# One pool for the weights of a whole decoder layer, and the down projection's operands kept in DRAM as high and low halves

## The chip, the cores and the metric

The kernel runs on one core of a Trainium2 chip. Its time is the device time of one execution in microseconds. Before the change the median of three runs is 2220.11 us (2217.4 to 2222.4). The profiled execution of the same kernel took 2217.63 us, of which the profile's span covers 2215.9 us.

## The reference

One layer of a hybrid decoder on 512 tokens of width 2048, all in fp32. Cut to what matters:

```python
h = rmsnorm(x, attn_pre_norm)
proj = h @ w_in                               # 2048 -> gated linear attention + differential attention
m = concat(gla(proj), diff_attention(proj)) @ w_o
x = x + rmsnorm(m, attn_post_norm)
h = rmsnorm(x, ffn_pre_norm)
up = h @ w_ffn_in                             # 2048 -> 2 x 5632
a, b = up[..., :5632], up[..., 5632:]
a = conv_w[0]*a[t-2] + conv_w[1]*a[t-1] + conv_w[2]*a[t] + conv_b
f = (gelu(a) * b) @ w_ffn_out                 # 5632 -> 2048
x = x + rmsnorm(f, ffn_post_norm)
```

The change touches how the weights of all these products are staged, and above all how gelu(a) * b travels from the up projection to the down projection.

## The kernel before

**Three products for one.** An fp32 value is split into a high half (ScalarE, ACT, copies it into the shorter type fp32r) and a low half (VectorE, DVE, subtracts the high half). A product is then three TensorE (PE) products: high by high, high by low, low by high. Weights arrive in *granules* of 128x1024 (512 KB) on SyncE's queue (SP); `granule` (L102) turns each into a pair "whi" (ACT, L111) and "wlo" (DVE, L112). `split` (L123) does the same for the moving operand: ACT at L124, DVE at L125. The moving operand of all stages lies in two resident tiles, "ah" and "al".

**Stages.** The input projections with both attentions run until about 690 us, then the output projection, a passage whose order is written out by hand (`to_ffn`), and `first_pair`, which makes the first 512 columns of the feed-forward net. From about 966 us come 20 *up units* (10 column groups, the gate branch and the linear branch of each), from about 1740 us 10 *down units*, and from about 2159 us a last part that adds the product of the first 512 columns and finishes the layer.

**A unit** computes a 2x2 block product with seven block products in place of eight, from sums of blocks. Its seven segments are called x0, z0, y0, z1, x1, y1 and y2, and each uses two granules and one of seven moving operands: a11, s5, s2, s3, a12, s7, a22, in that order. A granule is 24 products of 128x256 in an up unit (L888 to L890) and 12 of 128x512 in a down unit (L985 to L987). The weight sums are made by DVE (L853, L871) and by accumulating DMAs that GpSimd (POOL) issues (`more`, L837). Weights of a unit come into tiles "rt" (first block, four buffers) and "raw" (four buffers).

**From up to down.** After each unit of the linear branch `product` (L941) multiplies the two branches and `token_sums` writes the seven moving operands of the down stage to DRAM ("sd"): three are parts of the product, four are sums. `prepare` loads one such operand into a tile "st" and splits it into its place in "ah" and "al"; the down stage has 35 of these. Down products are accumulated in "acc" and "accp" by `into` (L991 on ACT, L993 on DVE).

**Pools.** "w" holds raw (4 buffers), whi and wlo (4 each) until the end of `first_pair`. It is then closed, and "w2" (rt 4, raw 4, whi and wlo 3 each) is opened in the same region. The working tiles of the up stage lie in a pool "fa"; when it is closed, those of the down stage come into "ff", in the same place. A tile in a pool that lies over an earlier one has to wait until the last reader of what lay there is done.

**What sets the order.** Outside the passages written by hand a scheduler that runs with a model of the engines orders each engine's queue; an engine then executes its queue strictly in order, SP's and POOL's queues of DMAs too.

## Time and profile before

| what | value |
|---|---|
| median of three runs | 2220.11 us |
| profiled execution | 2217.63 us |
| its span | 2215.9 us |
| mean granted TensorE clock | 0.991 |
| PE busy | 2148.3 us (97%) |
| DVE busy | 1421.0 us (64%) |
| ACT busy | 903.5 us (41%) |
| moved by DMA | 303.83 MB, 137 GB/s |

PE is the engine for which all else works. A row of the page's groups has line, engine, operation, output and inputs, then the count, the total busy time, the mean duration in ns, and the idle time of the engine just before these instructions with what ended it. Rows of a timeline have the start in us, the duration, and in brackets the idle time before, with its releaser. A row of the windows has the stretch, its length, the busy time and number of instructions of PE, its weight loads, DVE, ACT and POOL, the granted clock, the DMA engines' busy share and the rate in GB/s.

### The profile page before, as it was taken

The numbers are of one execution on the slowest core, as the hardware profiler recorded it, in microseconds if no ns is written. First come the engines' busy times: TensorE is split into PE (matmuls) and PEld (weight loads), VectorE is DVE, ScalarE is ACT, GpSimd is POOL, SyncE is SP. The second block draws the span as 40 slices with busy tenths as digits, with TensorE's granted clock in tenths as the row PEclk, the third lists the DMA queues.
The fourth block names the chain that finished last, engine by engine and source line by source line (L and its number), as shares of the span: only waits on it lengthen the run. The fifth ranks groups of instructions, "written<-read, shape, count | busy, mean of one in ns | idle before, by whom it ended". The sixth has DMA issues, their size and how long they took to land.

```text
span 2215.9 us, 31875 instructions
## 1 busy us (share of the span) xinstructions
PE 2148.3 (97%) x13009; PEld 1896.9 (86%) x13009; DVE 1421.0 (64%) x1721; ACT 903.5 (41%) x1162; POOL 204.4 (9%) x245
## 2 busy tenths in 40 slices
PE   7999999999999999999999999999999699999997
PEld 6778888877888889789999999999999588777786
DVE  5345553444453245857786777878778577887887
ACT  4233332333342234334554444454454364444442
POOL 1000000000000000011111111110111010110101
PEclk9999999999999999989999999999999899999999
DMA  6322222222224344175767667576766776676654
GB/s 208 111 67 77 76 77 76 77 77 85 77 88 168 96 143 162 40 180 138 161 150 184 145 156 183 131 163 159 175 154 148 224 220 160 167 190 155 166 128 144
DMA packets 218471, 303.83 MB, mean 137 GB/s; under 512 B 11776, under 2 KB 155572, under 8 KB 216404
## 3 DMA queue, kind: packets, MB, share of 16 engines
q1 hardware_dynamic: 165204, 238.87, 33.2%
q0 software_dynamic: 53120, 62.92, 18.3%
q8 instruction: 102, 1.67, 0.3%
q14 instruction: 45, 0.37, 0.1%
HBM read 273.97 MB, written 27.79 MB: 136 GB/s over the span
## 4 chain that ended last, share of the span: by engine, by line
PE 76%; issue 15%; DMA 4%; DVE 3%; POOL 1%; ACT 1%; SPq 0%; POOLq 0%; DVEq 0%; ACTq 0%
PE bank L888 11%; PE bank L890 11%; PE bank L889 11%; PE bank L165 6%; PE bank L167 6%; PE bank L166 6%; PE bank L149 5%; PE bank L147 5%; PE bank L148 5%; DMA raw<-in_w_ffn_out_dram 2%; PE bank L414 1%; DVE wlo L112 1%; PE bank L482 1%; PE bank L513 1%; PE bank L986 1%
## 5 line engine op out<-in xcount | busy, mean ns | idle before, releaser
L112 DVE TENSOR_TENSOR wlo<-raw,whi 128x1024 fp32r<-128x1024 f32 x325 | 396.1, 1223 | 380.7 <-ACT whi L111 380.0
L111 ACT ACTIVATE whi<-raw 128x1024 fp32r<-128x1024 f32 x325 | 343.8, 1059 | 625.0 <-PE bank L167 162.4
L112 DVE TENSOR_TENSOR wlo<-rt,whi 128x1024 fp32r<-128x1024 f32 x240 | 291.9, 1222 | 114.8 <-ACT whi L111 114.1
L111 ACT ACTIVATE whi<-rt 128x1024 fp32r<-128x1024 f32 x240 | 253.2, 1059 | 272.7 <-PE bank L889 177.7
L888 PE MATMUL bank<-ah,whi 128*128 128x256 f32 x1280 | 354.9, 277 | 4.8 <-ACT whi L111 4.8
L890 PE MATMUL bank<-ah,wlo 128*128 128x256 f32 x1280 | 354.7, 277 | 0.5 <-DVE wlo L112 0.5
L889 PE MATMUL bank<-al,whi 128*128 128x256 f32 x1280 | 354.5, 277 | 0.0
L165 PE MATMUL bank<-whi,ah 128*128 128x512 f32 x616 | 246.3, 401 | 0.2 <-ACT ah L124 0.2
L888 PEld LDWEIGHTS bank<-ah,whi 128*128 128x128 f32 x1280 | 241.6, 189 | 5.3 <-ACT whi L111 5.2
L166 PE MATMUL bank<-wlo,ah 128*128 128x512 f32 x616 | 242.7, 395 | 0.2 <-DVE wlo L112 0.2
L167 PE MATMUL bank<-whi,al 128*128 128x512 f32 x616 | 242.1, 395 | 0.0
L890 PEld LDWEIGHTS bank<-ah,wlo 128*128 128x128 f32 x1280 | 241.4, 189 | 0.8 <-DVE wlo L112 0.8
L889 PEld LDWEIGHTS bank<-al,whi 128*128 128x128 f32 x1280 | 241.5, 189 | 0.0
L986 PE MATMUL bank<-wlo,ah 128*128 128x512 f32 x560 | 222.0, 396 | 11.3 <-DVE wlo L112 11.2
L985 PE MATMUL bank<-whi,ah 128*128 128x512 f32 x560 | 198.8, 394 | 21.6 <-ACT ah L124 18.7
L987 PE MATMUL bank<-whi,al 128*128 128x512 f32 x560 | 219.6, 392 | 0.0
L147 PE MATMUL bank<-ah,whi 128*128 128x512 f32 (+1 forms) x528 | 202.4, 383 | 0.0
L148 PE MATMUL bank<-al,whi 128*128 128x512 f32 (+1 forms) x528 | 201.6, 382 | 0.0
L149 PE MATMUL bank<-ah,wlo 128*128 128x512 f32 (+1 forms) x528 | 200.6, 380 | 0.4 <-DVE wlo L112 0.4
L985 PEld LDWEIGHTS bank<-whi,ah 128*128 128x128 f32 x560 | 105.3, 188 | 46.4 <-ACT ah L124 19.1
L986 PEld LDWEIGHTS bank<-wlo,ah 128*128 128x128 f32 x560 | 105.5, 188 | 42.3 <-DVE wlo L112 19.9
L167 PEld LDWEIGHTS bank<-whi,al 128*128 128x128 f32 x616 | 116.1, 188 | 26.2 <-DVE al L125 0.3
(241 smaller groups left out, 3836.3 us busy)
## 6 DMA issues: line engine op xcount, KB each, us to landing
raw<-in_w_in_dram SPq DMA_DIRECT2D x96, 512.0 KB, 3.9
raw<-in_w_ffn_in_dram SPq DMA_DIRECT2D x96, 512.0 KB, 5.3
raw<-in_w_ffn_out_dram SPq DMA_DIRECT2D x48, 512.0 KB, 6.8
rt<-in_w_ffn_in_dram SPq DMA_DIRECT2D x40, 512.0 KB, 5.9
rt<-in_w_ffn_in_dram POOLq DMA_DIRECT2D x40, 512.0 KB, 5.9
raw<-in_w_ffn_in_dram POOLq DMA_DIRECT2D x40, 512.0 KB, 7.0
raw<-in_w_o_dram SPq DMA_DIRECT2D x32, 512.0 KB, 3.7
rt<-in_w_ffn_out_dram SPq DMA_DIRECT2D x20, 512.0 KB, 7.7
```

The costliest lines, as they stand in the source:

```text
L111: act(hi, raw, AF.Copy)
L112: tt(lo, raw, hi.bitcast(F32), ALU.subtract)
L147: mm(o, wh, ah[:, t0:t1, kk, :], start=st, stop=False)
L148: mm(o, wh, al[:, t0:t1, kk, :], start=False, stop=False)
L149: mm(o, wl, ah[:, t0:t1, kk, :], start=False, stop=sp)
L165: mm(banks[t], ah[:, t, s, :], w[0][:, k, :], start=st, stop=False)
L166: mm(banks[t], ah[:, t, s, :], w[1][:, k, :], start=False, stop=False)
L167: mm(banks[t], al[:, t, s, :], w[0][:, k, :], start=False, stop=sp)
L888: mm(o, wh, sh[:, :, kk, :], start=start and kk == 0 and n == 0, stop=False, **NOW)
L889: mm(o, wh, sl[:, :, kk, :], start=False, stop=False, **NOW)
L890: mm(o, wl, sh[:, :, kk, :], start=False, stop=kk == HK - 1, **NOW)
L986: mm(b[j], sh[:, o:o + P], w[1][:, q, :], start=False, stop=False, **NOW)
```

## The change

There are four parts.

1. *One pool.* "w" stays open for the whole kernel, with three buffers each of whi and wlo. The tiles rt get a pool of their own, "rp", opened after the output projection. A few granules of the first stages go to spare tiles: one in the first half of the mixer, one more each in `to_ffn`.
2. *In the down stage every fourth granule* is split into a pair "xhi"/"xlo" (one buffer) in "ff".
3. *The operands are split when they are written.* `put` splits each of the seven operands through one pair of tiles "oh" and "ol" (one buffer each) and writes both halves: 14 stores of 256 KB per token_sums where there were 7. The sums are now made in place in two buffers, and the order of the seven is a11, s5, s2, s3, a12, s7, a22. `prepare` becomes two loads straight into ah and al, with no tile st and no split. s2 and s3 of the first group are prepared earlier than before.
4. *The residual rows* of the last part are loaded into parts of ah and al that are free by then.

```diff
-    wstack = ExitStack()
-    wpool = wstack.enter_context(tc.tile_pool(name="w", bufs=4, side="right"))
+    wpool = ctx.enter_context(tc.tile_pool(name="w", bufs=3))
...
-            w[g] = granule(None, 2, raws[g])
+            w[g] = granule(None, 2, raws[g], spare=mx if g == 3 else None, bufs=1)
...
-            w[g] = granule(w_o3[:, order[2 * g]:order[2 * g] + 2, 1536:2048], 2, spare=wp if g > 4 else None)
+            w[g] = granule(w_o3[:, order[2 * g]:order[2 * g] + 2, 1536:2048], 2, spare=wp if g > 3 else None)
...
-        weights_f(wa, 0, 3)
+        weights_f(wa, 0, 3, wp)
...
+    rp = ctx.enter_context(tc.tile_pool(name="rp", bufs=4))
...
-    sd = [{n: dram.tile([P, 2, S], F32, name=f"sd{c}{n}") for n in SN} for c in range(NG // 2)]
+    sd = [{n: [dram.tile([P, 2, S], F32, name=f"sd{c}{n}{v}") for v in "hl"] for n in SN} for c in range(NG // 2)]
...
-    wstack.close()
-    wpool = ctx.enter_context(tc.tile_pool(name="w2", bufs=3, side="right"))
 
     def load_t(src, a):
-        raw = wpool.tile([P, GR], F32, name="rt", tag="rt", bufs=4)
+        raw = rp.tile([P, GR], F32, name="rt", tag="rt", bufs=4)
...
-                hl = granule(None, self.a, raws[g])
+                turn[0] += 1
+                hl = granule(None, self.a, raws[g], spare=ff if ff and turn[0] % 4 == 0 else None, bufs=1)
...
         def put(n, src):
-            dma(sd[c][n][:, i, :].rearrange("p (n t) -> p n t", n=2), src)
-
-        def add(n, x, y, op):
-            t = fp.tile([P, 2, 256], F32, name=n, tag="sum", bufs=4)
-            tt(t, x, y, op)
-            put(n, t)
-            return t
+            hl = [fp.tile([P, 2, 256], F32R, name=f"o{v}", tag=f"o{v}", bufs=1) for v in "hl"]
+            split(hl[0], hl[1], src)
+            for d, v in zip(sd[c][n], hl):
+                dma(d[:, i, :].rearrange("p (n t) -> p n t", n=2), v.bitcast(F32))
+
+        def total():
+            return fp.tile([P, 2, 256], F32, name="sum", tag="sum", bufs=2)
 
         put("a11", a11)
+        s = total()
+        tt(s, a21, a22, ALU.subtract)
+        put("s5", s)
+        tt(s, s, a11, ALU.subtract)
+        put("s2", s)
+        tt(s, s, a12, ALU.add)
+        put("s3", s)
         put("a12", a12)
+        s = total()
+        tt(s, a11, a21, ALU.subtract)
+        put("s7", s)
         put("a22", a22)
...
-    def prepare(c, n, stage=None):
-        raw = stage or ff.tile([P, GR], F32, name="st", tag="st", bufs=2)
-        dma(raw, sd[c][n].rearrange("p g x -> p (g x)"))
-        split(piece(ah, *place[n]), piece(al, *place[n]), raw)
+    def prepare(c, n):
+        for v, d in zip((ah, al), sd[c][n]):
+            dma(piece(v, *place[n]).bitcast(F32), d.rearrange("p g x -> p (g x)"))
...
             downs = [down_unit(c, cb) for c in range(NG // 2) for cb in range(2)]
+            prepare(0, "s2")
             downs[0].x0()
+            prepare(0, "s3")
             u.y2()
...
-            x1[t] = ff.tile([P, D], F32, name="x1", tag="x1", bufs=2)
+        x1 = {t: v[:, h].rearrange("p k c -> p (k c)").bitcast(F32)
+              for t, (v, h) in enumerate(((ah, 1), (al, 1), (ah, 2), (al, 2)))}
```

**The order at the opening of the up stage.** ACT's queue there, as it was. s5h, s2h and s3h are operands of the up units, "p" is the first up unit's evacuated product, and each whi made from rt belongs to an up unit.

```order
L124 ACTIVATE s5h<-u 128x1024
L124 ACTIVATE ah<-u 128x1024 x2
L740 ACTIVATE u<-u 128x512
L124 ACTIVATE s2h<-u 128x1024
L124 ACTIVATE s3h<-u 128x1024
L111 ACTIVATE whi<-rt 128x1024 x2
L909 ACTIVATE p_7080<-bank 128x512
L111 ACTIVATE whi<-rt 128x1024 x4
```

And with the change:

```order
L123 ACTIVATE s5h<-u 128x1024
L110 ACTIVATE whi<-rt 128x1024
L123 ACTIVATE ah<-u 128x1024 x2
L740 ACTIVATE u<-u 128x512
L110 ACTIVATE whi<-rt 128x1024 x2
L123 ACTIVATE s2h<-u 128x1024
L110 ACTIVATE whi<-rt 128x1024 x2
L911 ACTIVATE p_7114<-bank 128x512
L123 ACTIVATE s3h<-u 128x1024
L110 ACTIVATE whi<-rt 128x1024
```

Three splits of rt stand ahead of s2h now, and two more ahead of s3h, where both came before any of them.

**The order in the up stage.** ACT's queue over the last segments of one unit of the linear branch and the first of the next, as it was; whi is a weight granule, "u" and "p" are evacuated products.

```order
L909 ACTIVATE p_10624<-bank 128x512
L111 ACTIVATE whi<-rt 128x1024 x3
L111 ACTIVATE whi<-raw 128x1024 x6
L111 ACTIVATE whi<-rt 128x1024
L919 ACTIVATE u<-bank 128x2x256
L111 ACTIVATE whi<-rt 128x1024 x2
L737 ACTIVATE u<-u,cols 128x512 x2
L111 ACTIVATE whi<-rt 128x1024
```

And with the change, where "oh" is the high half that `put` writes, from the part "u" or the sum "sum":

```order
L123 ACTIVATE oh<-u 128x512
L110 ACTIVATE whi<-raw 128x1024 x2
L123 ACTIVATE oh<-sum 128x512
L110 ACTIVATE whi<-raw 128x1024 x2
L123 ACTIVATE oh<-sum 128x512
L110 ACTIVATE whi<-raw 128x1024
L123 ACTIVATE oh<-sum 128x512
L110 ACTIVATE whi<-raw 128x1024
L110 ACTIVATE whi<-rt 128x1024
L921 ACTIVATE u<-bank 128x2x256
L123 ACTIVATE oh<-u 128x512
L110 ACTIVATE whi<-rt 128x1024 x2
```

Splits for the stores now stand one by one between the splits of the weights; two more follow, with one granule of rt between, so that ACT handles 10 granules between the first and the last of the seven.

**The order from the up to the down stage.** ACT's queue, as it was:

```order
L124 ACTIVATE ah<-u 128x1024
L111 ACTIVATE whi<-rt 128x1024 x6
L111 ACTIVATE whi<-raw 128x1024
L991 ACTIVATE accp_15927<-bank 128x512
L991 ACTIVATE accp_15928<-bank 128x512
L991 ACTIVATE acc_15925<-bank 128x512
L991 ACTIVATE acc_15926<-bank 128x512
L124 ACTIVATE ah<-st 128x1024 x2
```

And with the change:

```order
L110 ACTIVATE whi<-rt 128x1024 x5
L123 ACTIVATE oh<-u 128x512
L123 ACTIVATE oh<-sum 128x512 x3
L123 ACTIVATE oh<-u 128x512
L123 ACTIVATE oh<-sum 128x512
L123 ACTIVATE oh<-u 128x512
L998 ACTIVATE accp_16291<-bank 128x512
L998 ACTIVATE accp_16292<-bank 128x512
L110 ACTIVATE xhi<-rt 128x1024
L110 ACTIVATE whi<-rt 128x1024
L110 ACTIVATE whi<-raw 128x1024 x2
L123 ACTIVATE ah<-st 128x1024
```

The seven splits of the last token_sums stand together ahead of the first down products' evacuation (accp), and behind that comes a granule split into xhi. The split of "st" that remains is the last part's operand, "ud0". SP's queue has the fourteen stores of these splits one behind the other, with no load between them, and ahead of them the last loads of operands of the first group:

```order
L48 DMA rt<-in_w_ffn_out_dram 128x2x512 x2
L48 DMA al<-sd0a22l 128x1024
L48 DMA ah<-sd0a22h 128x1024
L48 DMA sd4a11h<-oh 128x512
L48 DMA sd4a11l<-ol 128x512
L48 DMA sd4s5h<-oh 128x512
L48 DMA sd4s5l<-ol 128x512
L48 DMA sd4s2h<-oh 128x512
```

Before, SP had the loads of a22 and three others of the first group behind the last stores.

More of the change, by code (lines that the diff above doesn't have):

```diff
@@ L100, in load, with granule @@
         return raw
-    def granule(src, a, raw=None, spare=None, bufs=3):
+    def granule(src, a, raw=None, spare=None, bufs=4):
         if raw is None:
@@ L812, in hybrid_layer @@
     drain()
[L813 to L814 removed]
     def load_t(src, a):
[L817 removed]
+        raw = rp.tile([P, GR], F32, name="rt", tag="rt", bufs=4)
         dma(raw.rearrange("p (a b) -> p a b", a=a), src)
         return raw
+    turn = [0]
+    ff = None
     class Unit:
@@ L1027, in hybrid_layer @@
         if nxt is None:
-            prepare(0, "a11", pair_tile().rearrange("p n t -> p (n t)"))
+            prepare(0, "a11")
         u.x1()
         if nxt is None:
-            prepare(0, "s5", pair_tile().rearrange("p n t -> p (n t)"))
+            prepare(0, "s5")
         u.y1()
@@ L1054, in hybrid_layer @@
         last_cb = i % 2 == 1 and nxt is not None
-        if first:
+        if first and i:
             prepare(i // 2, "s3")
@@ L1113, in last_group @@
         rs = {}
-        x1 = {}
-        def residual_row(t):
-            x1[t] = ff.tile([P, D], F32, name="x1", tag="x1", bufs=2)
+        x1 = {t: v[:, h].rearrange("p k c -> p (k c)").bitcast(F32)
+              for t, (v, h) in enumerate(((ah, 1), (al, 1), (ah, 2), (al, 2)))}
+        for t in range(NT):
             dma(x1[t], x1d[t])
```

9 lines of the change are left out of this document (removed).

## Prediction

> **What bounds the kernel now.** I read the page's first part, then the windows by stage, PE's waits, the timelines at PE's two long gaps, and the groups of the last long stage.
>
> ```profile
> PE 2148.3 (97%) x13009; PEld 1896.9 (86%) x13009; DVE 1421.0 (64%) x1721; ACT 903.5 (41%) x1162; POOL 204.4 (9%) x245
> ```
>
> PE is busy for 97% of the span and the change leaves every matmul in place, so only time that PE loses can be gained. The windows say where it loses any.
>
> ```profile
> core 0: us, PE busy (x) PEld busy (x) DVE busy (x) ACT busy (x) POOL busy (x), PEclk, DMA share, GB/s
> 936.60:965.60 29.00, 19.38 (x114) 18.59 (x114) 14.88 (x15) 8.95 (x9) 2.77 (x2) 0.76 0.76 199
> 1000.00:1700.00 700.00, 700.00 (x6027) 700.00 (x6026) 529.84 (x538) 328.13 (x359) 92.42 (x72) 1.00 0.68 160
> 1744.50:1767.00 22.50, 3.82 (x11) 3.01 (x11) 7.61 (x9) 5.24 (x7) 1.19 (x1) 0.62 0.73 248
> 1776.00:2150.00 374.00, 360.38 (x1549) 288.62 (x1548) 298.83 (x313) 170.71 (x174) 43.37 (x36) 1.00 0.66 172
> 2100.00:2150.00 50.00, 50.00 (x220) 41.04 (x219) 40.08 (x44) 19.84 (x19) 5.68 (x5) 1.00 0.60 137
> ```
>
> The up stage (second row) loses nothing: 6027 matmuls in 700 us, 0.1161 us each. At that pace the 114 of the opening (first row) need 13.2 us, so 15.8 of its 29 are lost. A down-stage matmul takes 50/220 = 0.227 us where PE never waits; the boundary's 11 need 2.5, so 20.0 are lost, and 1549 need 352, so about 22 of the down stage's 374 are lost. These 58 us are all that the change can win.
>
> ```profile
> PE bank L985 <- ACT ah L124: 18.7, 1, 18.7
> PE bank L986 <- DVE wlo L112: 11.2, 14, 1.6
> PE bank L888 <- ACT whi L111: 8.7, 2, 4.8
> SPq L48 <- DVE wlo L112: 1281.1, 277, 26.7
> SPq L48 <- PE bank L149: 18.4, 1, 18.4
> ```
>
> (Columns: total, times, longest.) The first row is the boundary, the second the down stage, the third the opening.
>
> **The change part by part.** *The opening.* The tiles "rt" lie in a pool that opens over "w"; the last row above is SP holding their first load for 18.4 us until the last product of an earlier user of that place is done.
>
> ```profile
> 936.64 0.92 SPq L48 DMA_DIRECT2D rt<-in_w_ffn_in_dram  x2
> 941.39 0.58 PE L888 MATMUL bank<-ah,whi 128*128 128x256 f32 x1 [4.78 <-ACT whi L111]
> 954.32 0.58 PE L888 MATMUL bank<-s5h,whi 128*128 128x256 f32 x1 [3.92 <-ACT whi L111]
> ```
>
> The load goes out at 936.64 and PE, which needs it, restarts at 941.39. With "w" never closed, and "rt" where tiles lay that have long been read, these loads need not wait. Both gaps go, and with them the low clock (0.76) behind them: -15.8. DVE's 14.9 us of work there lay partly in the gaps and is now beside products; I give back 1.5. Result -14.3; bounds -8 (the second gap, which hangs on accumulating loads as well, stays) and -16.
>
> *Three buffers of whi/wlo in place of four in the mixer.*
>
> ```profile
> L111 ACT ACTIVATE whi<-raw 128x1024 fp32r<-128x1024 f32 x325 | 343.8, 1059 | 625.0 <-PE bank L167 162.4
> ```
>
> ACT idles mostly until PE frees a buffer, so it is ahead by all four; with three it is still two granules ahead of the one in use, about 11 us (a granule there is 24 products of 0.23), against 1.1 + 1.2 for a split. I take +1, bounds 0 and +4.
>
> *The put chain in the up stage.* Nine of the ten token_sums now issue, beside products, seven splits through one pair of tiles "oh"/"ol": split n waits until store n-1 has landed. ACT's splits stand in its queue between those of the weights, so a late store delays weights. From the first "oh" to the last ACT handles 10 granules, each 24 x 0.1161 = 2.79 us of PE: 27.9 us for six hops. A hop is one 128x512 ACT pass (0.59, quoted below) and one landing.
>
> ```profile
> sd0s<-s SPq DMA_DIRECT2D x8, 256.0 KB, 3.3
> sd2s<-s SPq DMA_DIRECT2D x8, 256.0 KB, 2.0
> sd4s<-s SPq DMA_DIRECT2D x8, 256.0 KB, 3.5
> sd0a<-u SPq DMA_DIRECT2D x6, 256.0 KB, 5.8
> sd1a<-u SPq DMA_DIRECT2D x6, 256.0 KB, 5.5
> sd4a<-u SPq DMA_DIRECT2D x6, 256.0 KB, 5.6
> ```
>
> Weighted, these medians give 4.1, so a hop is 4.7 and six are 28.2 us: the slots, almost exactly. ACT's lead of two granules (5.6) is the reserve, so landings may average (27.9 + 5.6)/6 - 0.59 = 5.0 before PE waits. DVE gains 63 passes of 0.68, 43 us on 530: 82% of the 700. The doubled stores add 18 MB to 160 GB/s x 700 us = 112 MB, so the DMA share goes from 0.68 to about 0.79. I take +4 (a microsecond in about every second group); bounds 0 and +33 (landings all at 5.6: six hops 37.1, less 27.9 and 5.6, nine times).
>
> The Trainium skill ("DMA: Bandwidth & Descriptors", section "Anatomy of one DMA — SWDGE (gpsimd) path") speaks against such a chain: a transfer has a fixed part of about 2.0 us, mostly the receipt of the last write, and its fit 2.0 + bytes/436e3 gives, as an estimate, 2.6 us for 256 KB. The trace's 2.0 agrees with the floor. By it alone six hops are 19 us, this term 0 and the sum 4 lower; the rows above say that stores behind loads take twice that, and the rows decide.
>
> *The boundary.*
>
> ```profile
> 1739.76 0.68 DVE L927 TENSOR_TENSOR u<-bank,p 128x512 f32<-128x512 f32 x1
> 1741.49 1.22 DVE L941 TENSOR_TENSOR u<-u 128x1024 f32<-128x1024 f32 x1
> 1745.61 4.40 SPq L48 DMA_DIRECT2D sd4s<-s  x4
> 1756.08 1.09 ACT L991 ACTIVATE accp<-bank 128x512 f32<-128x512 f32 x2 [10.38 <-DMA sd4s<-s]
> 1762.12 1.06 ACT L124 ACTIVATE ah<-st 128x1024 fp32r<-128x1024 f32 x1 [3.98 <-DMA st<-sd0s]
> 1763.23 0.80 PE L985 MATMUL bank<-whi,ah 128*128 128x512 f32 x1 [18.68 <-ACT ah L124]
> ```
>
> Call 1739.76 T. Before: the product at T+3.0, stores to T+10, pool "fa" free at T+16.3, then the load and split of s2, PE at T+23.5. Now s2 is loaded early, but the second granule of z0 goes to "xhi" in "ff", which lies over "fa" and must wait for the whole put chain. After T PE has the rest of y2 and a granule or two, so it stops much as before. The chain: T+3.0; seven hops, the first behind two late operand loads (5.6 + 0.6), six with little beside them (2.1 + 0.6): 22.4; the last "ol" pass and its store 0.7; two accp passes 1.2, the xhi pass 1.1: PE at T+28.4, 4.9 later than before. One more for a DVE queue that has wlo passes heaped up behind the chain: +6. Bounds: all hops at the floor and no heap, +1; hops of 4.1 + 0.6 throughout, 10 more: +16.
>
> *The down stage.*
>
> ```profile
> L125 DVE TENSOR_TENSOR al<-st,ah 128x1024 fp32r<-128x1024 f32 x31 | 37.8, 1221 | 10.2 <-ACT ah L124 9.7
> L124 ACT ACTIVATE ah<-st 128x1024 fp32r<-128x1024 f32 x31 | 32.8, 1056 | 31.5 <-PE bank L986 21.1 <-DMA st<-ud 6.2 <-DMA st<-sd0a 4.2
> L991 ACT ACTIVATE accp<-bank 128x512 f32<-128x512 f32 x2 | 1.2, 590 | 0.5 <-PE bank L987 0.5
> ```
>
> These 37.8 us of DVE and 32.8 of ACT go. What they cost PE now:
>
> ```profile
> 1782.24 0.50 PE L986 MATMUL bank<-wlo,ah 128*128 128x512 f32 x1 [0.20 <-DVE wlo L112]
> 2090.07 1.22 DVE L125 TENSOR_TENSOR al<-st,ah 128x1024 fp32r<-128x1024 f32 x1
> 2091.20 2.35 DVE L112 TENSOR_TENSOR wlo<-rt,whi 128x1024 fp32r<-128x1024 f32 x2
> 2092.48 0.51 PE L986 MATMUL bank<-wlo,ah 128*128 128x512 f32 x1 [1.21 <-DVE wlo L112]
> ```
>
> The first and the last of the 14 waits for wlo. In 11 of them, 9.7 of 11.2 us, an "al" pass stands just ahead of the wlo awaited, as in the two DVE rows. The named waits do not make up the 22 lost; taking the same share of the whole (0.87) gives -19 at most. But 31 more loads of 0.52 MB (16 MB in 374 us, 43 GB/s on 172) lift the DMA share from 0.66 to about 0.83, and accumulating loads, which set the other waits, come later for it. I take -14; bounds -8 and -19. One buffer pair in four is the single "xhi", which waits for its own last reader four granules (11 us) back, as a fourth buffer would.
>
> *The tail.* The rows of x1 come into free parts of ah/al ahead of the end; 0.
>
> Sum on the profiled execution: -14.3 + 1 + 4 + 6 - 14 = -17.3 on 2217.6, so 2200.3. The median of the runs lies 2.5 above that execution: 2202.8, say **2202**.
>
> **The rivals.** *R1, the put chain bounds the up stage.* With loads between stores on SP, every landing is the 5.5 of sd1a: six hops are 36.5, less 27.9 and the 5.6 of lead, 3.0 per group, 27 in nine: 2202 - 4 + 27 = 2225; with 5.8 it is 2242, so 2232 in the middle. It decides from a landing of 5.0 on. For it: three of six rows are above that. Against it: sd2s and sd0s stand at 2.0 and 3.3 amid the same loads.
>
> *R2, only the opening is won.* Chain hops of 4.7 at the boundary (+16), and a down stage that the doubled loads hold back (-8): 2202 + 10 + 6 = 2218; with only one of the two 2208 to 2212, so 2211. For it: sd4s, the very stores of the boundary, have 3.5. Against: SP has no other load between these stores.
>
> *R3, the opening isn't released*, as its second gap hangs on an accumulating load and the sums s2 and s3 move into PE's time: +9, 2211, and 2216 if neither gap goes. Against it: ACT now has the first rt splits ahead of those of s2 and s3.
>
> **How the numbers follow.** The forecast has 0.50, with a range of its own of 2192 to 2210; R2 0.25, R1 0.15, R3 0.10. 2187 (boundary at +1, down stage at -19, put chain at 0 and the opening at -15) to 2226 (R1's lower end) leaves out most of R1 and little at the bottom. A measurement of this kernel tells about 0.2%, 4.4 us, from no change. Faster by more: all of the forecast, 0.21 of R2 and 0.05 of R3, 0.76. Within: 0.03 of R2, 0.04 of R3, 0.07. Slower: R1 and 0.02 of the others, 0.17.
>
> **What would show it.** Right: in the opening's window no PE wait above 1 us and a granted clock near 1.00; one PE wait of 20 to 25 us at the boundary, released by xhi, with seven store landings of 2 to 3 us in a row before it; fewer than five waits for wlo in the down stage, and less than 10 us lost there; DVE at about 82% and PE at 100% in the up stage. Wrong: "oh" or "ol" waiting for sd stores while PE waits for whi in each second unit (R1); a boundary wait above 30 us or down-stage waits for loads of ah, raw or rt (R2); rt still awaited at the opening (R3).

## The result and the profile after

The changed kernel takes 2269.05 us (median of four runs, 2268.16 to 2269.78) against 2219.95 us for the kernel before, measured beside it: a ratio of 1.022, with a 95% interval of 1.020 to 1.024. It is 49 us slower, where 18 us faster was forecast. R1, the put chain, is what happened, and it costs 69.7 us where R1 gave it 27 to 44.

PE's line of the page and the windows of the changed kernel, in the stages shown of before (columns as there; the last row begins 20 us after PE's restart at the boundary):

```profile
PE 2165.8 (96%) x13009; PEld 1912.9 (84%) x13009; DVE 1418.8 (63%) x1756; ACT 903.2 (40%) x1197; POOL 205.2 (9%) x245
```

```profile
934.00:966.00 32.00, 32.00 (x253) 31.00 (x252) 25.50 (x26) 13.59 (x14) 3.85 (x3) 1.00 0.58 117
1000.00:1700.00 700.00, 658.86 (x5491) 654.28 (x5490) 509.85 (x544) 326.89 (x382) 84.85 (x66) 0.98 0.67 167
1066.00:1072.00 6.00, 6.00 (x40) 6.00 (x41) 5.97 (x7) 4.09 (x7) 0.00 (x0) 0.74 0.40 131
1795.00:1832.00 37.00, 10.93 (x38) 7.84 (x38) 16.52 (x20) 9.69 (x14) 0.00 (x0) 0.65 0.69 256
1847.25:2207.25 360.00, 357.41 (x1549) 289.94 (x1548) 267.51 (x286) 142.09 (x145) 41.78 (x35) 1.00 0.77 219
```

The opening (first row) is closed: PE is busy for the whole of it, at a granted clock of 1.00. The up stage, which lost nothing before, has 5491 products in the 700 us that held 6027. The boundary is longer, and the down stage has 1549 products in 360 us. The answering row of the kernel before, again 20 us after its restart, has 1490:

```profile
1783.23:2143.23 360.00, 346.57 (x1490) 277.57 (x1490) 289.60 (x304) 164.19 (x167) 43.37 (x36) 1.00 0.65 167
```

PE's waits in the changed kernel (total, times, longest):

```profile
PE bank L892 <- DVE wlo L111: 44.5, 17, 5.6
PE bank L992 <- ACT xhi L110: 25.9, 2, 25.5
PE bank L890 <- ACT whi L110: 1.5, 4, 0.7
PE bank L993 <- DVE xlo L111: 1.5, 2, 0.8
```

L890 and L892 are the first and third products of an up triple, L992 and L993 are in a down unit. The first row was 0.9 us before, the second takes the place of the wait for ah, and the last is what is left of the 14 waits for wlo (11.2 us) in the down stage.

The stages end to end, from the first and last start of their products. The line of the first product of an up triple, in the kernel before and then in the changed one (count, shortest, median and longest in ns, first and last start):

```profile
L888 PE MATMUL bank<-ah,whi x1280: 276/276/582, 941.4 to 1738.6; 128*128 128x256 f32 x183
```

```profile
L890 PE MATMUL bank<-ah,whi x1280: 276/276/420, 939.1 to 1794.9; 128*128 128x256 f32 x183
```

The last part ends with PE's last first-of-three product at 2201.6 us before and 2252.6 us after. The up units begin with the first up product, at 941.4 before, and not at the 966 us given above; the opening is their first 25 us. With the restarts at 1763.23 and 1827.25, each behind 48 down products, that gives this account:

| stretch | before | after | difference |
|---|---|---|---|
| to the first up product | 941.4 | 939.1 | -2.3 |
| first to last up product | 797.2 | 855.8 | +58.6 |
| last up product to restart | 24.6 | 32.4 | +7.8 |
| restart to the last part's end | 438.4 | 425.3 | -13.1 |

One group of the up stage shows the mechanism. Rows of ACT's timeline in the changed kernel:

```profile
1026.54 0.61 ACT L123 ACTIVATE oh<-u 128x512 fp32r<-128x512 f32 x1
1038.01 0.62 ACT L123 ACTIVATE oh<-sum 128x512 fp32r<-128x512 f32 x1
1040.30 1.06 ACT L110 ACTIVATE whi<-raw 128x1024 fp32r<-128x1024 f32 x1 [1.67 <-PE bank L892]
1046.89 0.63 ACT L123 ACTIVATE oh<-sum 128x512 fp32r<-128x512 f32 x1 [5.52 <-DMA sd0s2h<-oh]
1055.64 0.63 ACT L123 ACTIVATE oh<-sum 128x512 fp32r<-128x512 f32 x1 [2.04 <-DMA sd0a12h<-oh]
1057.59 1.04 ACT L110 ACTIVATE whi<-rt 128x1024 fp32r<-128x1024 f32 x1
1063.66 0.63 ACT L123 ACTIVATE oh<-u 128x512 fp32r<-128x512 f32 x1 [5.03 <-DMA sd0s7h<-oh]
```

DVE and PE at the same place:

```profile
1061.88 0.69 DVE L124 TENSOR_TENSOR ol<-sum,oh 128x512 fp32r<-128x512 f32 x1 [4.75 <-DMA sd0a12l<-ol]
1064.47 1.22 DVE L111 TENSOR_TENSOR wlo<-rt,whi 128x1024 fp32r<-128x1024 f32 x1
1065.74 0.58 PE L892 MATMUL bank<-ah,wlo 128*128 128x256 f32 x1 [4.80 <-DVE wlo L111]
```

ACT has the granule's high half ready at 1058.6, but its low half waits behind an "ol" that DVE may not write until the store of a12 has landed, 4.75 us after DVE came to it. Three passes of the convolution (to 1064.55) stand between that ol and the wlo, and PE stops for 4.80. From the first "oh" of this group (1026.54) to the last (1063.66) the seven splits take 37.1 us, where the ten granules between them are 27.9 us of PE's work. In all nine groups it is 35.0 to 37.6, in the mean 36.4.

The six hops are not alike. The first two take 5.8 and 5.7 us in each group, with no wait for a store: two granules' splits stand in each and wait for PE. The third and the sixth, with one granule each (2.79 us of PE), take 8.5 and 7.4 in the mean, and the two between, with two granules each, 4.3 and 4.7. The landings differ in the same way. Medians of stores of single operands, as far as the profile has them:

```profile
sd1s5h<-oh SPq DMA_DIRECT2D x2, 256.0 KB, 2.0
sd0s2h<-oh SPq DMA_DIRECT2D x2, 256.0 KB, 8.1
sd0s7h<-oh SPq DMA_DIRECT2D x2, 256.0 KB, 7.3
```

The third hop waits for the store of s2 and the sixth for that of s7. Why these two land so late is not shown.

### The profile page after: what moved, and what is told of

It is laid out like the page before. It is cut to its first block, busy times and chain, and to the rows that moved or that the text cites. A ratio compares the mean times of both kernels' runs of the same rounds, so it can differ in the third digit from the quotient of the medians.

```text
span 2266.9 us, 32200 instructions
## 1 busy us (share of the span) xinstructions
PE 2165.8 (96%) x13009; PEld 1912.9 (84%) x13009; DVE 1418.8 (63%) x1756; ACT 903.2 (40%) x1197; POOL 205.2 (9%) x245
## 4 chain that ended last, share of the span: by engine, by line
PE 58%; issue 30%; DMA 4%; POOL 3%; DVE 2%; ACT 1%; SPq 0%; POOLq 0%; DVEq 0%; ACTq 0%
PE bank L164 6%; PE bank L166 6%; PE bank L165 6%; PE bank L148 5%; PE bank L146 5%; PE bank L147 5%; PE bank L892 4%; PE bank L890 4%; PE bank L891 4%; PE bank L993 2%; PE bank L994 2%; PE bank L992 2%; POOL rt L839 1%; POOL raw L839 1%; PE bank L413 1%
## 5 line engine op out<-in xcount | busy, mean ns | idle before, releaser
L111 DVE TENSOR_TENSOR wlo<-raw,whi 128x1024 fp32r<-128x1024 f32 x307 | 373.7, 1222 | 384.9 <-ACT whi L110 375.7
L110 ACT ACTIVATE whi<-raw 128x1024 fp32r<-128x1024 f32 x307 | 324.6, 1058 | 586.0 <-PE bank L166 160.3
L892 PE MATMUL bank<-ah,wlo 128*128 128x256 f32 x1280 | 363.5, 284 | 44.6 <-DVE wlo L111 44.5
L890 PE MATMUL bank<-ah,whi 128*128 128x256 f32 x1280 | 361.3, 282 | 1.6 <-ACT whi L110 1.5
L111 DVE TENSOR_TENSOR wlo<-rt,whi 128x1024 fp32r<-128x1024 f32 x220 | 268.2, 1221 | 110.3 <-ACT whi L110 110.0
L110 ACT ACTIVATE whi<-rt 128x1024 fp32r<-128x1024 f32 x220 | 231.1, 1056 | 232.6 <-PE bank L891 134.9
L892 PEld LDWEIGHTS bank<-ah,wlo 128*128 128x128 f32 x1280 | 247.6, 193 | 48.6 <-DVE wlo L111 48.6
L890 PEld LDWEIGHTS bank<-ah,whi 128*128 128x128 f32 x1280 | 247.5, 193 | 2.7 <-ACT whi L110 2.5
L164 PE MATMUL bank<-whi,ah 128*128 128x512 f32 x600 | 238.5, 401 | 0.6 <-ACT ah L123 0.6
L166 PE MATMUL bank<-whi,al 128*128 128x512 f32 x600 | 236.7, 396 | 0.0
L165 PE MATMUL bank<-wlo,ah 128*128 128x512 f32 x600 | 236.7, 395 | 0.0
L994 PE MATMUL bank<-whi,al 128*128 128x512 f32 x420 | 165.2, 393 | 0.0
L993 PE MATMUL bank<-wlo,ah 128*128 128x512 f32 x420 | 164.7, 392 | 0.5 <-DVE wlo L111 0.5
L992 PE MATMUL bank<-whi,ah 128*128 128x512 f32 x420 | 162.1, 391 | 0.6 <-issue 0.6
L165 PEld LDWEIGHTS bank<-wlo,ah 128*128 128x128 f32 x600 | 113.3, 189 | 25.1 <-DVE wlo L111 0.5
L164 PEld LDWEIGHTS bank<-whi,ah 128*128 128x128 f32 x600 | 113.4, 189 | 24.4 <-ACT ah L123 1.0
```

The costliest lines, as they stand in the source:

```text
L110: act(hi, raw, AF.Copy)
L111: tt(lo, raw, hi.bitcast(F32), ALU.subtract)
L164: mm(banks[t], ah[:, t, s, :], w[0][:, k, :], start=st, stop=False)
L165: mm(banks[t], ah[:, t, s, :], w[1][:, k, :], start=False, stop=False)
L166: mm(banks[t], al[:, t, s, :], w[0][:, k, :], start=False, stop=sp)
L890: mm(o, wh, sh[:, :, kk, :], start=start and kk == 0 and n == 0, stop=False, **NOW)
```

## The experiments

Durations are of the up stage (first to last up product), of the boundary (last up product to restart) and the median; the kernel before has 797.2, 24.6 and 2219.95, the changed one 855.8, 32.4 and 2269.05. Stretches are of one profiled execution, which can lie some us off the median: 3.2 below it with two buffers for both halves, 6.5 above it where the oh stores of that kernel go by ACT's queue. Every kernel gets a queue order of its own from the scheduler, so a run can differ from its base in more than the lines shown.

**The operands written in fp32 and split on loading, all else as changed.** `put`, `add` and `prepare` are those of before, with the order of the sums and their four buffers, and s2 and s3 of the first group are prepared as late as they were.

```diff
-            hl = [fp.tile([P, 2, 256], F32R, name=f"o{v}", tag=f"o{v}", bufs=1) for v in "hl"]
-            split(hl[0], hl[1], src)
-            for d, v in zip(sd[c][n], hl):
-                dma(d[:, i, :].rearrange("p (n t) -> p n t", n=2), v.bitcast(F32))
+            dma(sd[c][n][:, i, :].rearrange("p (n t) -> p n t", n=2), src)
...
-        for v, d in zip((ah, al), sd[c][n]):
-            dma(piece(v, *place[n]).bitcast(F32), d.rearrange("p g x -> p (g x)"))
+        raw = stage or ff.tile([P, GR], F32, name="st", tag="st", bufs=2)
+        dma(raw, sd[c][n].rearrange("p g x -> p (g x)"))
+        split(piece(ah, *place[n]), piece(al, *place[n]), raw)
```

> The seven operands are written in fp32 and split when they are loaded, as before the change; the one pool, the spare granules and the residual rows stay as in the change. Theory 1 (the single pair oh/ol: its seven splits in a row stop the queues of ACT and DVE until stores land, 8 to 9 us for each of nine groups): the up stage is back at about 78 us per group with no PE wait for wlo above 1 us, the opening stays closed, the down stage loses about 20 us again; 2195 to 2210. Rival A (fewer weight buffers and pools are what costs the up stage): the waits of 4 to 5 us in each second unit stay, 2245 or more.

Measured: 2176.87 us, a ratio of 0.981 to before (0.978 to 0.984). It is the fastest kernel of this study, 42 us below the kernel before (2219.30 beside it). The up stage takes 786.1, the boundary 11.2. Its rows of the up product, of the opening and of the down stage:

```profile
L890 PE MATMUL bank<-ah,whi x1280: 276/276/286, 938.6 to 1724.7; 128*128 128x256 f32 x183
```

```profile
934.00:966.00 32.00, 32.00 (x255) 31.09 (x254) 25.85 (x25) 13.11 (x13) 3.85 (x3) 1.00 0.58 120
1755.95:2115.95 360.00, 360.00 (x1568) 294.08 (x1567) 306.83 (x321) 174.60 (x176) 42.97 (x36) 1.00 0.70 185
```

So the put chain with all that hangs on it costs 855.8 - 786.1 = 69.7 us of the up stage; rival A falls. The expectation missed on the other side: it had the down stage lose about 20 us again with the splits of operands back on ACT and DVE, but it holds 1568 products in 360 us, more than the changed kernel without those splits. That made a new question of the prediction's reason for the down stage.

**Two buffers for one half only.** `oh` with two and `ol` with one, and the reverse; `sum` goes to one buffer to make room.

```diff
-            hl = [fp.tile([P, 2, 256], F32R, name=f"o{v}", tag=f"o{v}", bufs=1) for v in "hl"]
+            hl = [fp.tile([P, 2, 256], F32R, name=f"o{v}", tag=f"o{v}", bufs=2 if v == "h" else 1) for v in "hl"]
...
-            return fp.tile([P, 2, 256], F32, name="sum", tag="sum", bufs=2)
+            return fp.tile([P, 2, 256], F32, name="sum", tag="sum", bufs=1)
```

> The change with two buffers for oh, one for ol, and one for sum in place of two. Theory 1: ACT no longer stops for the store just ahead, DVE still does for ol; about half of the up stage's 75 us comes back, 2225 to 2245. Rival B (the doubled stores take the DMA engines' time, and weights come late whatever the splits wait for): within 5 us of 2269.

> The change with two buffers for ol, one for oh, and one for sum in place of two. Theory 1: DVE no longer stops, ACT still does; 2225 to 2245, and the PE waits that stay are for whi. Rival B: within 5 us of 2269.

Measured: 2262.81 us with two of oh (up stage 853.5) and 2250.22 with two of ol (842.3). Both are misses as to size: freeing one queue gives back 2 and 14 us of 70, not half. The kind of wait came as expected. PE's waits in the up stage (966 to 1700 us), with two of oh and then with two of ol:

```profile
PE bank L892 <- DVE wlo L111: 37.2, 14, 5.6
```

```profile
PE bank L890 <- ACT whi L110: 24.8, 16, 3.4
PE bank L892 <- DVE wlo L111: 3.7, 7, 0.8
```

With DVE still held, PE waits for wlo; with ACT still held, for whi. The first of the two runs is the telling one. With two of oh, ACT's waits of oh for stores fall from 86 to 28 us (966 to 1720 us) and its six hops from 36.4 to 28.3 us, about the 27.9 that the prediction allowed. DVE's waits for stores stay (51 and 46), with the same number of granules between its splits, and so does nearly the whole loss: DVE's chain alone is enough. With two of ol DVE has no such wait left and ACT has 91 us of them, so ACT's chain alone costs most of it too.

**Two buffers for both halves.** `sum` one buffer, `u` five in place of six.

```diff
-            hl = [fp.tile([P, 2, 256], F32R, name=f"o{v}", tag=f"o{v}", bufs=1) for v in "hl"]
+            hl = [fp.tile([P, 2, 256], F32R, name=f"o{v}", tag=f"o{v}", bufs=2) for v in "hl"]
...
-            return fp.tile([P, 2, 256], F32, name="sum", tag="sum", bufs=2)
+            return fp.tile([P, 2, 256], F32, name="sum", tag="sum", bufs=1)
...
-        return fp.tile([P, 2, S], F32, name="u", tag="u", bufs=6)
+        return fp.tile([P, 2, S], F32, name="u", tag="u", bufs=5)
```

> The change with two buffers each for oh and ol, one for sum, and five for u in place of six to make room. Theory 1: the splits wait for the store two before, and the up stage is back near 78 us per group; 2193 to 2212, unless the fifth u buffer is missed, which would show as waits for u. Rival B: 2260 or more.

Measured: 2213.56 us, a ratio of 0.998 to before (0.997 to 0.999), up stage 810.1. Of the 70 us, 46 come back. That is the largest piece of the answer: the single pair of tiles. The scheduler also placed the splits otherwise: on ACT 1, 3, 1, 0, 1 and 1 granules stand between the seven, where the changed kernel has 2, 2, 1, 2, 2 and 1. The 46 us are those of the buffers with this order; no run holds the order fixed. PE's waits in the up stage (966 to 1700 us) are now short, but not gone:

```profile
PE bank L892 <- DVE wlo L111: 12.2, 15, 1.1
```

**The splits without stores behind them.** The kernel of the first experiment with seven more splits per token_sums, into one oh and one ol that nothing reads, and five u.

```diff
             dma(sd[c][n][:, i, :].rearrange("p (n t) -> p n t", n=2), src)
+            hl = [fp.tile([P, 2, 256], F32R, name=f"o{v}", tag=f"o{v}", bufs=1) for v in "hl"]
+            split(hl[0], hl[1], src)
```

> The run with the operands split on loading, with seven more splits per token_sums into one oh and one ol that nothing stores, and five u buffers to make room for them: the engines' work of the change's splits, without a store to wait for. Theory 1 (what costs is waiting for stores to land): the up stage stays within 4 us of 786, 2173 to 2181. Rival D (0.6 us of ACT and 0.7 us of DVE in front of the weights' splits are the cost): the up stage gets 20 us or more longer, as in the run with two of each, which took 810.

Measured: 2186.28 us, and the up stage takes 786.2, as without them:

```profile
L890 PE MATMUL bank<-ah,whi x1280: 276/276/286, 939.1 to 1725.3; 128*128 128x256 f32 x183
```

The engines' work of the splits is free beside the up products, and five u buffers are as good as six; rival D falls. The median is above the range, since the boundary takes 16.9 where it took 11.2, and the restart to the end 427.6 where it took 424.3.

**The stores without the splits.** The kernel of the first experiment, every store issued a second time to another place.

```diff
-            dma(sd[c][n][:, i, :].rearrange("p (n t) -> p n t", n=2), src)
+            for d in (sd, sd2):
+                dma(d[c][n][:, i, :].rearrange("p (n t) -> p n t", n=2), src)
```

> The run with the operands split on loading, with each of its seven stores per token_sums issued twice, to a second place in DRAM: the change's number of stores and bytes, with no split to wait for them. Theory 1: the up stage within 4 us of 786, and the boundary a few us longer for seven more stores, 2176 to 2184. Rival B (the traffic of the doubled stores makes weights late): the up stage 15 us or more longer.

Measured: 2189.04 us, up stage 792.7. Twice the stores cost the up stage 6.6 us, more than the 4 expected and well below rival B's 15; the boundary, 15.5 us, puts the median above the range. So 63 of the 70 us need split and store together.

**The stores on ACT's queue.**

```diff
-                dma(d[:, i, :].rearrange("p (n t) -> p n t", n=2), v.bitcast(F32))
+                nc.scalar.dma_start(out=d[:, i, :].rearrange("p (n t) -> p n t", n=2), in_=v.bitcast(F32))
```

> The change with the fourteen stores of each token_sums issued from ACT's queue in place of SP's; one buffer each for oh and ol as in the change. Theory 1a (a store is late because it stands on SP's queue behind weight loads, and the loads behind the stores are held up in turn): landings of 2 to 4 us, the up stage loses less than half of its 70 us, 2200 to 2235. Theory 1b (it is the shared DMA engines that make a store late, on whatever queue): landings still 4 to 8 us, 2255 or more.

Measured: 2256.48 us, up stage 846.1. The landing of the oh stores (shortest, median, longest, in us; the profile has it for 23 of the 70 in each), in the changed kernel and then with ACT's queue:

```profile
DMA to landing us min/median/max: 2.0/3.5/8.5
```

```profile
DMA to landing us min/median/max: 2.0/4.4/7.9
```

Landings are as late as on SP, so theory 1a falls. The weight loads that stand ahead on SP's queue are not what makes a store late.

**Fewer splits behind a store.** oh with three buffers; ol, one buffer, is used by s5 and s2 alone, and the low halves of the rest go over the sum or the part itself (order s5, s2, s3, s7, a11, a12, a22; u with five buffers).

```diff
-        def put(n, src):
+        def put(n, src, own=True):
-            hl = [fp.tile([P, 2, 256], F32R, name=f"o{v}", tag=f"o{v}", bufs=1) for v in "hl"]
-            split(hl[0], hl[1], src)
-            for d, v in zip(sd[c][n], hl):
+            h = fp.tile([P, 2, 256], F32R, name="oh", tag="oh", bufs=3)
+            l = src.bitcast(F32R) if own else fp.tile([P, 2, 256], F32R, name="ol", tag="ol", bufs=1)
+            split(h, l, src)
+            for d, v in zip(sd[c][n], (h, l)):
```

> The change with fewer splits behind a store: three buffers for oh, one for ol that only s5 and s2 use, and the low halves of the other five written over the sum or the part itself, whose last use that is (their order is now s5, s2, s3, s7, a11, a12, a22; five u buffers). Theory 1 (waiting for stores is the cost, traffic 7 us, the engines' work 0): the up stage between 793 (no wait left) and 803, against 810 with two of each and 856 with one; 2190 to 2206. If the up stage stays at 810 or more, something else than the number of buffers holds the splits. Either way not below old_put's 2177, whose up stage is 786.

Measured: 2223.96 us, up stage 821.1; a miss. DVE no longer waits for any store in the up stage, and ACT's waits on stores add up to 34 us, as with two of each. But ACT waits 94 us for weight loads there. Its rows, of this kernel and then of the first experiment (966 to 1720 us):

```profile
ACT whi L110 <- DMA rt<-in_w_ffn_in_dram: 51.2, 19, 5.7
ACT whi L110 <- DMA raw<-in_w_ffn_in_dram: 42.7, 15, 4.5
```

```profile
ACT whi L110 <- DMA raw<-in_w_ffn_in_dram: 32.8, 10, 3.9
```

Such waits need not cost much: with every store issued twice ACT waits 80 us for loads in the same stretch, and the up stage is 6.6 us longer. Why more loads are late here was the next question.

**The same with the stores on GpSimd's queue, and two of each with the oh stores on ACT's.**

```diff
-                dma(d[:, i, :].rearrange("p (n t) -> p n t", n=2), v.bitcast(F32))
+                nc.gpsimd.dma_start(out=d[:, i, :].rearrange("p (n t) -> p n t", n=2), in_=v.bitcast(F32))
```

> As in_place, with all fourteen stores issued from GpSimd's queue, so that SP has weight loads alone. Theory 2 (what in_place still loses, 821 against 793, is weight loads that stand on SP behind stores that wait for their splits: ACT waits 94 us for loads there, 33 in old_put): the up stage goes to 793 to 803 and ACT's waits for loads to 30 to 60 us, 2190 to 2206, unless the accumulating loads, now behind stores on GpSimd's queue, come late in their turn. Rival B2 (the stores' traffic makes the loads late on whatever queue): the up stage stays at 815 to 825.

```diff
-            for d, v in zip(sd[c][n], hl):
-                dma(d[:, i, :].rearrange("p (n t) -> p n t", n=2), v.bitcast(F32))
+            for d, v, q in zip(sd[c][n], hl, (nc.scalar, nc.sync)):
+                q.dma_start(out=d[:, i, :].rearrange("p (n t) -> p n t", n=2), in_=v.bitcast(F32))
```

> As both2_u5, with the seven stores of the high halves issued from ACT's queue right behind their splits, those of the low halves from SP. Theory 2: SP is held for half as many stores, and the up stage goes from 810 to about 800, 2200 to 2207. Rival B2: within 3 us of 810.

Measured: 2247.51 us (up stage 843.3) and 2228.34 (829.5). Both are longer than with all stores on SP, which neither theory gave; the first expectation had only named late accumulating loads as an exception. On GpSimd's queue the stores stand in front of the accumulating loads. One of its waits there, in the up stage (966 to 1720 us; total, times, longest):

```profile
POOL sd1s5h L958 <- ACT oh L123: 35.5, 2, 18.1
```

A store that waits up to 18 us for its split holds the queue, and ACT still waits 51 us for rt. So theory 2 isn't shown, and moving the stores is no remedy. What the last 17 us with two of each are (810.1 against 792.7) stays open: 14 of them are PE's short waits for wlo, and what makes those low halves late is not shown.

**The down stage: the fourth buffer.** First the changed kernel without the spare pair there, then the kernel before with nothing but the spare pair.

```diff
-                hl = granule(None, self.a, raws[g], spare=ff if ff and turn[0] % 4 == 0 else None, bufs=1)
+                hl = granule(None, self.a, raws[g], spare=None, bufs=1)
```

> The change without the spare pair in the down stage, so three buffers of whi/wlo there; operands still loaded straight into place. Theory of the prediction (the al and ah passes are what made PE wait for wlo): the part from the end of the boundary to the end of PE's work stays at about 425 us, no more than 5 waits for wlo. Rival C (the fourth buffer is what helps, as the run with the operands split on loading, which has it, had no wait there): it goes back to about 438, with more than ten waits for wlo or whi.

```diff
-                hl = granule(None, self.a, raws[g])
+                turn[0] += 1
+                hl = granule(None, self.a, raws[g], spare=ff if ff and turn[0] % 4 == 0 else None, bufs=1)
```

> The kernel before with one thing of the change: every fourth granule of the down stage is split into the spare pair. Rival C: the down stage loses its 14 waits for wlo and 12 to 20 us, 2200 to 2210. Theory of the prediction: the al passes still stand ahead of wlo, the waits stay for the most part, 2214 to 2221.

Measured: 2282.99 us without the pair (ratio to before 1.029), and 2191.56 us for the kernel before with the pair (0.988, 0.986 to 0.990). Without the pair the part from the restart on takes 427.7 us, between the two forecasts, but that restart comes 24 products (5.5 us) later in the program; its 10 waits for wlo and 5 for whi are those of rival C. So equal stretches of time are compared. The same 360 us of the down stage in the two, each 20 us after its restart:

```profile
1855.58:2215.58 360.00, 352.05 (x1512) 281.26 (x1511) 262.89 (x280) 138.51 (x140) 41.38 (x35) 1.00 0.75 215
```

```profile
1770.61:2130.61 360.00, 359.92 (x1566) 293.71 (x1565) 305.00 (x320) 173.94 (x176) 42.96 (x36) 1.00 0.68 179
```

The kernel before has 1490 products there. Taking the operand splits away gives 22 more, 5 us at 0.23 each; the fourth buffer alone gives 76, 17 us, with every operand split still in DVE's queue. In the changed kernel the pair gives 37 (1549 against 1512), 8.5 us. Rival C holds, and the second run came out better than rival C had it because the boundary became shorter too: 12.2 us in place of 24.6.

**The boundary.** The kernel of the first experiment with s2 of the first group prepared before the last up segment, and the spare pair's turn moved to the second granule of y0, and then to the first.

```diff
-    turn = [0]
+    turn = [2]
...
+            prepare(0, "s2", pair_tile().rearrange("p n t -> p (n t)"))
             downs[0].x0()
...
-    prepare(0, "s2")
     downs[0].z0()
```

> The run with the operands split on loading (one pool, spare granules), with s2 of the first group loaded and split ahead of the last up segment, and the spare pair's turn moved on by two granules, so that the first down granule that has to wait for the up stage's tiles is the second of y0, not of z0. Expected: PE's wait of 8 us at the boundary goes down to 0 to 3, and the clock stays up: 2166 to 2174, against 2177. Rival: the wait only moves by two granules with its cause (the last stores landing), and the time stays at 2177.

```diff
-    turn = [0]
+    turn = [3]
```

> As early_s2, but the first down granule that waits for the up stage's tiles is the first of y0, one granule sooner. Expected, if accumulating loads in flight are what made the last stores land late there (7 us after the issue, against 2 in old_put): ACT still splits two granules of z1 ahead, so they are in flight here too, and the wait is as long, 14 to 17 us, 2179 to 2184. If the place of the granule alone decides: 11 us or less, 2174 to 2178.

Measured: 2180.86 us (ratio 0.983, 0.981 to 0.985) and 2181.38. The first is a miss, and worse than its rival. PE's wait in the first experiment's kernel, and with s2 early:

```profile
PE bank L987 <- ACT xhi L110: 8.0, 1, 8.0
```

```profile
PE bank L987 <- ACT xhi L110: 14.1, 1, 14.1
```

The second has 12.9, between its two cases; its time is that of the first case. In the kernel of the first experiment ACT is let go 2.2 us after SP issued the last of the stores:

```profile
1729.38 2.25 SPq L48 DMA_DIRECT2D sd4s<-s  x4
1733.87 1.08 ACT L993 ACTIVATE accp<-bank 128x512 f32<-128x512 f32 x2 [9.37 <-DMA sd4s<-s]
```

With s2 early it is 7.3 us. Two accumulating loads have been issued since 1732, SP adds a load of raw at 1737.47, and the profile names a load of raw, not a store, as what ACT waited for last:

```profile
1732.83 1.19 POOL L839 DMA_DIRECT2D raw<-in_w_ffn_out_dram  x1 [17.98 <-DVE wlo L111]
1734.57 1.20 POOL L839 DMA_DIRECT2D raw<-in_w_ffn_out_dram  x1 [0.55 <-DVE wlo L111]
1733.16 4.22 SPq L48 DMA_DIRECT2D sd4s<-s  x4
1744.73 1.09 ACT L993 ACTIVATE accp<-bank 128x512 f32<-128x512 f32 x2 [9.98 <-DMA raw<-in_w_ffn_out_dram]
```

In the kernel before there is one such load, and ACT is let go 6.1 us after the last store (1750.0 to 1756.08):

```profile
1748.15 1.19 POOL L837 DMA_DIRECT2D raw<-in_w_ffn_out_dram  x1 [19.04 <-DVE wlo L112]
```

One reading is that the loads hold the stores up: where PE stops sooner, the splits behind stop too, no accumulating load starts, and the stores land fast. The fourth trace fits it badly. With the turn at the first granule of y0 two accumulating loads were issued as well (1733.13 and 1736.60), and ACT is let go 4.3 us after the last store (1737.25 to 1741.52), sooner than with the one of the kernel before. So the cause is open; no run moves the loads alone.

## Why the prediction was wrong

**The opening** (-14.3): right. The first up product comes 2.3 us sooner, and in the first experiment the up stage is 11.1 us shorter, together 13 to 14; the window has no PE wait. Its rival R3 did not happen.

**Three buffers in the mixer** (+1): within its bounds, not isolated. It lies within the 939.1 us to the first up product, which comes without the gap of 4.8 us that stood there before, and so some 2.5 us later than it would. No run takes this part alone, and in the runs with it that point lies anywhere from 937.6 to 939.7.

**The put chain in the up stage** (+4, bounds 0 and +33): this is the step that failed. It measured +69.7, of which 6.6 are the traffic of twice the stores, 46 come back with a second buffer of each tile, and 17 stay open. The mechanism was named, as R1, and four parts of its pricing were wrong:

- *The hop.* The sum took one landing for all stores, the weighted median of before, 4.1 us, and so 28.2 us for six hops. They took 36.4 in the mean, within 0.1 of R1's 36.5. That agreement is luck: R1 had six equal hops with a landing of 5.5 in each, and the first two hops here wait for no store at all, while the stores of s2 and s7 land after 6.7 to 8.1 (medians).
- *The slots.* Six hops were set against ten granules as one sum. But the late stores stand where one granule lies between two splits: the third and the sixth hop overrun their 2.79 us by 5.7 and 4.6 in the mean, the first two, paced by PE, save nothing for them, and the two between save 2.2 of their 11.2.
- *The reserve.* The prediction counted ACT's chain alone, with 5.6 us of lead. By its own formula hops of 36.4 cost 2.9 per group, 26 in nine; PE's waits are 46. PE waits for wlo (44.5) and hardly for whi (1.5), so it was DVE's tile that ended the waits, and the run with two of oh shows DVE's chain to be enough. The sign that the prediction gave for R1 named whi.
- *The clock.* PE's waits in the up stage are 46 us of the 70. Most of the rest is slower products behind them. The 6 us behind the wait that ends at 1065.74 hold 38 products, where 52 fit at 0.1161; the 6 us behind each of the nine waits of 2.49 us and more hold 327 together, where 465 fit, which makes 16 us. The prediction has the low clock behind a gap in its term for the opening, and none in this one.

**The boundary** (+6): right in its chain. It measured +7.8. The chain was forecast to let PE go at 28.4 us after the last segment's evacuation (1739.76 before), and it is 28.4 (1798.82 to 1827.25). Three of ACT's seven splits there:

```profile
1801.81 0.63 ACT L123 ACTIVATE oh<-u 128x512 fp32r<-128x512 f32 x1 [4.16 <-DVE u L943]
1806.73 0.63 ACT L123 ACTIVATE oh<-sum 128x512 fp32r<-128x512 f32 x1 [4.29 <-DMA sd4a11h<-oh]
1820.96 0.63 ACT L123 ACTIVATE oh<-u 128x512 fp32r<-128x512 f32 x1 [2.10 <-DMA sd4s7h<-oh]
```

One hop of 4.9 behind the late operand loads, which the prediction gave 6.2, and five of 2.7 to 3.2, which it gave 2.7. So the chain lets PE go 4.9 us later than before, as forecast. The rest of the +7.8 is not the heap of wlo passes that the prediction added (+1): the evacuation itself starts 3.9 us after the last up product, and 1.2 before.

**The down stage** (-14): the size is right (-13.1), the reason for the most part not, so the size is luck. The prediction gave the whole gain to the splits of operands that go from DVE and ACT; of the spare pair it said that it waits as a fourth buffer would, and gave it no price. The down stage before had three buffers and has four with the pair. On the way to the changed kernel the splits bring 5 us and the pair 8.5. The pair alone, with all splits in place, brings 17, and taking the splits away then brings nothing (1549 products in place of 1566). An "al" pass stands ahead of wlo in most of the 14 waits, and that costs PE something only while the fourth buffer is missing. The doubled loads took the DMA share to 0.77, not the 0.83 worked out, and with four buffers held nothing up: the run with two of oh and ol has 1567 products in its 360 us.

**The tail** (0): nothing in the account speaks against it; no run takes the residual rows alone.

The rivals: R1 had its place right, and its price, 27 to 44, was too low by a factor of 1.6 to 2.6 for the reasons above. Its condition, landings above 5.0 in the mean, can't be read off: the profile has a third of the landings of oh, half of them at 3.5 us or less. Its chance of 0.15 rested on the quick medians, sd2s and sd0s, as evidence against it.

## What to carry to other kernels

A tile that is split into, stored and split into again ties the queues that write it to the landing of a store. With one buffer, set each hop, with a slow landing of the rows and not their median, against the work that stands in that hop, not the sum of the hops against the sum of the work. Do it for every in-order queue that waits there (here two), and ask what stands behind it. When a delay is seen in front of a wait, ask whether one more buffer removes the wait before the work in front of it is moved: here the spare pair alone brought 27 us, and moving the work cost more than it freed.

## What the runs showed of the hardware that was not expected

A store of 256 KB lands 2.0 to 8.5 us after its issue in the changed kernel, and from ACT's queue no sooner (2.0 to 7.9). The Trainium skill ("DMA: Bandwidth & Descriptors", section "Anatomy of one DMA — SWDGE (gpsimd) path") has a fixed part of about 2.0 us and, as an estimate from its fit, 2.6 for this size, for DMAs that GpSimd issues. These stores are issued by SP; their shortest landing lies below that estimate, and their longest is three times it.

PE's granted clock falls behind waits of 2.5 us as it does behind waits of 4.8. Three of the up stage's shorter waits in the changed kernel, and the 6 us from the end of each (columns of the last three rows as in the windows):

```profile
1324.29 0.39 PE L892 MATMUL bank<-ah,wlo 128*128 128x256 f32 x1 [3.11 <-DVE wlo L111]
1666.27 0.41 PE L892 MATMUL bank<-ah,wlo 128*128 128x256 f32 x1 [2.49 <-DVE wlo L111]
1565.55 0.38 PE L892 MATMUL bank<-ah,wlo 128*128 128x256 f32 x1 [0.76 <-DVE wlo L111]
1324.29:1330.29 6.00, 6.00 (x37) 6.00 (x38) 5.24 (x6) 3.49 (x5) 0.00 (x0) 0.72 0.57 190
1666.27:1672.27 6.00, 6.00 (x37) 6.00 (x38) 4.26 (x5) 4.48 (x7) 0.00 (x0) 0.72 0.68 208
1565.55:1571.55 6.00, 6.00 (x52) 6.00 (x53) 2.91 (x3) 2.70 (x4) 2.57 (x2) 1.00 0.79 204
```

The first product misleads: after 3.11 us it takes 0.39, like the one after 0.76. But about 1 us later the products behind it slow down, and the 6 us hold 37, as behind the wait of 2.49; behind the 4.80 shown further up they hold 38. Behind 0.76 they hold 52, at a granted clock of 1.00. So a wait of 2.49 us cost, as an estimate from these counts, 1.7 us more in slow products, and one of 4.80 cost 1.6. Between 0.76 and 2.49 us this up stage has no wait. The Trainium skill ("TensorE: Matmul & The Clock Gate", section "HAM oscillation — how this bites in real kernels") gives idle gaps of more than about 3.4 us as the bound. The trace does not agree: the waits of 2.49 and 3.11 lie below it, and the clock fell behind both.
